# Summing four gate-weight tiles on GpSimd earlier in the start-up of a hybrid attention layer, and bunching the other four

## The chip, the cores and the metric

The kernel runs on one core of a Trainium2 chip. The metric is device time in microseconds (us) from the first to the last instruction of a launch with what the runtime adds around it; lower is better. Of the kernel before there are three timed runs and one profiled execution.

The engines are named as the profile names them: PE is TensorE (matrix products; PEld is its weight load), DVE is VectorE, ACT is ScalarE, POOL is GpSimd, and SP is the engine that issues most DMAs. Each works through its own instructions in a fixed order and waits on semaphores.

## The reference

One post-norm residual sub-layer over `x` of 1024 rows by 1024 columns, all in float32. A conditioning vector `c` gives shift, scale and a residual gate; the normalised rows go through one wide projection, then through eight heads of forgetting attention and eight of stick-breaking attention, and back through an output projection. What matters here is the gate:

```
mod = silu(c) @ w_ada + b_ada
shift, scale, gate = mod[:, :D], mod[:, D:2*D], mod[:, 2*D:]
u = layer_norm(x) * (1 + scale) + shift
h = u @ w_in                      # q, k, v, g of both head groups
...                               # two kinds of attention, gated by silu(g)
resid = ALPHA * x + gate * (y @ w_out)
out = layer_norm(resid, ln_g, ln_b)
```

The gate is a vector of 1024 numbers: the product of `silu(c)` (1024 long) and a 1024 by 1024 block of `w_ada`. It is first needed when the output weights are scaled by it, far into the kernel.

## The kernel before

**Products.** Every product is made of three float32r products: the operands are split into a high part and a rest (hi and lo), and hi times hi, hi times lo and lo times hi are summed in PSUM. PE is the engine with the most work.

**Start-up.** The input projection of the first head pair and the q and k of the second is written out by hand. The five outputs in `START` (named q0, k0, g0, q1, k1 in the tiles) are computed in two passes: a first pass over rows 0 to 511, and a second pass over rows 512 to 1023. In the second pass `late_round(kb)` (L717) transposes a block of normalised rows on PE, ACT writes its high part `uh` (L219) and the modulated block itself (L220), and DVE the rest `ul` (L223). `start_steps` (L558) then runs three products per weight tile (L567, L568, L571). The first two accumulators, both halves of `late_acc` and named `st_late` in the profile (q and k of pair 0), are filled together (L740). The third (`st_g0b`), fourth (`st_q1b`) and fifth (`st_k1b`) are filled one after the other by the loop at L749. Each accumulator is read out by `evac_m` in two halves of heads: ACT rounds a q or k half (L232, L241), DVE takes the rest (L233, L244), and for k an SP DMA copies the half to the other partitions (L243). Within one accumulator these steps alternate: an ACT half waits for the DVE half before it.

**The gate.** `load_gate(kt)` (L689) fetches one of eight weight tiles of 128 rows by 1024 columns (`wg`, 512 KB) into the pool `att`, which has six buffers and holds the input rows `x` before and the attention tiles `kp` and `be` after. `gate_term(kt, h)` (L693) adds `silu(c)` times one half (512 columns) of a tile to the tile `gate`. Half 0 goes over ACT (scale, L698) and POOL (add, L699); half 1 is one DVE instruction (L701); for tile 0 ACT writes both halves (L696). The loads of tiles 0 to 3 are issued during the second pass (L742), and those of tiles 4 to 7 in the loop at L749, one every three steps. The eight terms themselves also stand in that loop, at every third of its 24 steps, under `after(*rounded)`, which lets them be placed only behind the last rounding of the second pass. At L713 one product then sums `gate` over the partitions.

**What sets the order.** PE and SP follow the order in which the code is written up to L767, and PE to the end. The orders of ACT, DVE and POOL, and of SP after L767, are chosen ahead of time by a scheduler, so a changed line can move instructions elsewhere.

**What follows.** The first attention units run beside the projection of v for rows 512 on: scores `S` (L411, L412), of which there is one buffer; ACT makes `kp` and `be` from it (L430, L431); DVE scans `kp` (L436); POOL clears one column of `be` and multiplies (L443, L442); PE transposes `be` (L459). Beside it POOL splits fetched weights into `whi` (L125) and `wlo` (L126): `v_2b` and `v_3b` for the v projection, then `2_0` and `2_1` (the g weights of pair 1).

Of the kernel before, what the change touches and what calls it, by code (L numbers as in the profile page):

```python
# [10 lines left out]
AF = mybir.ActivationFunctionType  # L11
ALU = mybir.AluOpType
# [4 lines left out]
NB = 8  # L17
# [10 lines left out]
def tile_hybrid_layer(  # L28
# [17 lines left out]
    nc = tc.nc  # L46
# [9 lines left out]
    def att_tile(name, dt=F32):  # L56
        return big("att", 6, name, dt)
# [15 lines left out]

    RING = 5
    WARM = (4, 1, 1, 1, 1)
    GEARLY = 8
    NORM_ON = {6: nc.vector, 7: nc.vector}
    FROW = 12
    SPACE = 5
# [2 lines left out]
    def after(*instructions):  # L82
        stack = ExitStack()
        for i in instructions:
            stack.enter_context(tc.issue_after(i.ins))
        return stack
# [17 lines left out]
    gate = cp.tile([P, D], F32, tag="gate", name="gate")  # L104
# [53 lines left out]
    sc = cp.tile([P, NB], F32, tag="sc", name="sc")  # L158
# [113 lines left out]
    def evac_m(p, m, ch, acc, heads=(0, 1)):  # L272
        if m == 0:
            evac_q(p, ch, acc, qst[p], heads)
        elif m == 1:
            return evac_k(p, ch, acc, kst[p], klo[p], heads)
        else:
            evac_g(p, ch, acc, sgt[p])
# [279 lines left out]
    def start_steps(ns, accs, kb, a=0, b=512, parts=(0, 1)):  # L558
        s = slice(a, b)
        w = {}  # L560
        for n in ns:
            hi, lo = split[("k", kb) if n < NW else ("h", kb // 4)]
            at = n if n < NW else kb % 4
            w[n] = hi[:, at * P:at * P + P], lo[:, at * P:at * P + P]
        if 0 in parts:
            for n in ns:
                nc.tensor.matmul(accs[n], w[n][0], u_hi[kb][:, s], start=(kb == 0), stop=False)  # L567
                nc.tensor.matmul(accs[n], w[n][1], u_hi[kb][:, s], start=False, stop=False)  # L568
        if 1 in parts:
            for n in ns:  # L570
                nc.tensor.matmul(accs[n], w[n][0], u_lo[kb][:, s], start=False, stop=(kb == NB - 1))  # L571
# [115 lines left out]
    wg = {}  # L687

    def load_gate(kt):  # L689
        wg[kt] = att_tile(f"wg_{kt}")  # L690
        nc.sync.dma_start(wg[kt], w_gate[kt])

    def gate_term(kt, h):  # L693
        s = slice(h * 512, h * 512 + 512)
        if kt == 0:
            nc.scalar.activation(gate[:, s], wg[kt][:, s], AF.Copy, scale=sc[:, 0:1])  # L696
        elif h == 0:
            nc.scalar.activation(wg[kt][:, s], wg[kt][:, s], AF.Copy, scale=sc[:, kt:kt + 1])  # L698
            nc.gpsimd.tensor_tensor(gate[:, s], gate[:, s], wg[kt][:, s], op=ALU.add)  # L699
        else:  # L700
            nc.vector.scalar_tensor_tensor(gate[:, s], wg[kt][:, s], sc[:, kt:kt + 1], gate[:, s],  # L701
                                           op0=ALU.mult, op1=ALU.add)
# [14 lines left out]
    def late_round(kb):  # L717
        u_turn(kb, 512, 1024)
        return u_round(kb, 512, 1024), u_rest(kb, 512, 1024)
# [17 lines left out]
    for kb in range(NB):  # L737
        if kb + 2 < NB:
            rounded = late_round(kb + 2)
        start_steps(range(2), acc1, kb, 512, 1024)  # L740
        if kb < 4:
            load_gate(kb)  # L742
        if kb < len(evacs):
            n, h = evacs[kb]
            with after(*rounded):
                evac_m(*START[n], 0, acc0[n], (h,))
    acc1 += [pv_tile("st_g0b", True), pv_tile("st_q1b"), acc_tile("st_k1b")]
    v0_w.update((n, fetch_w(f"v0_{n}b", w_v[0, n], 512)) for n in (2, 3))
    for n in range(5):  # L749
        if n >= 2:  # L750
            for kb in range(NB):
                start_steps((n,), acc1, kb, 512, 1024)
                step = (n - 2) * NB + kb
                if step % 3 == 1 and step // 3 < GEARLY:
                    with after(*rounded):
                        gate_term(step // 3, 0)
                        gate_term(step // 3, 1)
                    if step // 3 < 4:
                        load_gate(step // 3 + 4)
        last_evac = evac_m(*START[n], 1, acc1[n])  # L760
        if n == 2:
            floor.append(ps.tile([P, 512], F32, tag="fl", bufs=1, name="floor"))
            nc.vector.memset(floor[0][:, :512 - P], 0.0)
            nc.scalar.copy(floor[0][:, 512 - P:], ident)
# [282 lines left out]
```

## Time and profile before

| | us |
|---|---|
| timed runs, lowest / median / highest of 3 | 698.71 / 699.13 / 699.32 |
| profiled execution, its own time | 699.99 |
| its span, first to last instruction | 698.2 |
| PE busy in the span | 676.0 (97%) |
| POOL busy | 410.6 (59%) |
| DVE busy | 483.7 (69%) |
| ACT busy | 385.0 (55%) |

A line of the timeline gives the start, the duration (of a run of equal instructions: from the first start to the last end), the engine, the line of the kernel, the operation, the tiles written and read, the shapes and the count, and in brackets how long the engine had been idle and what released it. A line of the chain of waits gives a start, a duration and what the chain went through. The rows that carry the argument are in the prediction.

### The profile page before, as it was taken

How to read it: one execution, taken by the hardware profiler on the slowest of the kernel's cores; microseconds unless marked ns; L12 is line 12 of the kernel's file. 1: busy time of each engine (PE TensorE's matmuls, PEld its weight loads, DVE VectorE, ACT ScalarE, POOL GpSimd, SP SyncE). 2: the span in 40 equal slices, each digit the busy share in tenths (PEclk: the TensorE clock that was granted, in tenths of full speed). 3: DMA queues.
4: the chain of work that ended last, by engine and by line, in shares of the span. 5: the costliest groups of instructions: out<-in, count | busy, mean ns of one | idle time of the engine just before them, and what ended most of it. 6: DMA issues, size and time to landing. Idle time of an engine off the chain costs nothing.

```text
span 698.2 us, 11781 instructions
## 1 busy us (share of the span) xinstructions
PE 676.0 (97%) x4033; PEld 589.0 (84%) x4033; DVE 483.7 (69%) x931; ACT 385.0 (55%) x866; POOL 410.6 (59%) x530
## 2 busy tenths in 40 slices
PE   7999989999999999999999999999999999999995
PEld 4789887888997888889988877889988889888884
DVE  5985678767657676767686684758576767784644
ACT  5667567856658576666664554645564666531000
POOL 4560487656437566556388897868483464665412
PEclk9999999999999999999999999999999999999998
DMA  8953451112102122112144554345241299143301
GB/s 313 415 215 128 113 176 53 28 39 49 42 9 69 40 53 55 38 46 61 29 134 145 174 164 155 112 116 164 95 143 51 58 283 364 56 162 113 119 31 60
DMA packets 44027, 81.59 MB, mean 117 GB/s; under 512 B 5120, under 2 KB 18880, under 8 KB 43072
## 3 DMA queue, kind: packets, MB, share of 16 engines
q1 hardware_dynamic: 42816, 76.65, 33.5%
q10 hardware_dynamic: 1152, 4.19, 2.0%
q8 instruction: 32, 0.52, 0.3%
q14 instruction: 27, 0.22, 0.1%
HBM read 60.34 MB, written 16.29 MB: 110 GB/s over the span
## 4 chain that ended last, share of the span: by engine, by line
PE 76%; DVE 7%; DMA 5%; POOL 4%; ACT 4%; issue 3%; SPq 0%; POOLq 0%; DVEq 0%; ACTq 0%
PE pv L474 9%; PE m L256 8%; PE m L257 8%; PE m L258 8%; PE T L459 8%; PE o L835 4%; PE o L833 4%; PE o L834 4%; PE S L412 4%; PE S L411 4%; PE v L311 3%; PE v L313 3%; PE v L312 3%; DMA wss<-in_w_ss_dram 1%; DMA raw<-in_w_qkg_dram 1%
## 5 line engine op out<-in xcount | busy, mean ns | idle before, releaser
L256 PE MATMUL m<-uh,whi 128*128 128x512 f32 x304 | 126.3, 415 | 0.5 <-DVE kl L244 0.5
L257 PE MATMUL m<-ul,whi 128*128 128x512 f32 x304 | 119.8, 394 | 0.0
L258 PE MATMUL m<-uh,wlo 128*128 128x512 f32 x304 | 119.6, 394 | 0.0
L462 DVE TENSOR_TENSOR pt<-T,pt 128x512 fp32r<-128x512 f32 (+2 forms) x192 | 100.6, 550 | 16.1 <-ACT pt L461 14.9
L442 POOL TENSOR_TENSOR be<-be,kp 128x127 f32<-128x127 f32 (+3 forms) x64 | 77.1, 1205 | 34.9 <-DVE kp L440 25.9
L461 ACT CAST pt<-T 128x512 fp32r<-128x512 f32 (+2 forms) x192 | 85.7, 480 | 17.2 <-PE T L459 13.6
L436 DVE TENSOR_TENSOR_SCAN kp<-kp,floor 128x512 f32<-128x512 f32 (+2 forms) x64 | 65.2, 1018 | 32.4 <-ACT kp L430 31.4
L474 PE MATMUL pv<-pt,v 128*128 128x256 f32 (+3 forms) x640 | 81.7, 272 | 3.8 <-DVE pt L462 3.8
L474 PEld LDWEIGHTS pv<-pt,v 128*128 128x128 f32 (+1 forms) x640 | 77.4, 163 | 9.0 <-DVE pt L462 4.7
L425 POOL TENSOR_SCALAR a<-a,l 128x1024 f32<-128x1024 f32 (+3 forms) x64 | 48.3, 755 | 43.8 <-DVE l L424 31.2
L423 ACT ACTIVATE a<-a,nm 128x1024 f32<-128x1024 f32 (+3 forms) x64 | 49.8, 778 | 40.5 <-DVE nm L418 40.1
L258 PEld LDWEIGHTS m<-uh,wlo 128*128 128x128 f32 x304 | 57.1, 188 | 13.5
L411 PE MATMUL S<-k,q 128*128 128x512 f32 (+5 forms) x192 | 66.6, 348 | 1.5 <-ACT be L431 0.8
L412 PE MATMUL S<-kl,qz 128*128 128x512 f32 (+5 forms) x192 | 65.5, 342 | 0.0
L256 PEld LDWEIGHTS m<-uh,whi 128*128 128x128 f32 x304 | 57.3, 188 | 9.2 <-DVE kl L244 0.9
L257 PEld LDWEIGHTS m<-ul,whi 128*128 128x128 f32 x304 | 57.4, 189 | 8.0
L495 POOL TENSOR_TENSOR ty<-ty,sg 64x256 f32<-64x256 f32 x64 | 47.7, 745 | 26.5 <-DVE ty L494 12.5
L418 DVE CUSTOM_DVE_ANT_0 a<-S,fb 128x1024 f32<-128x1024 f32 (+3 forms) x64 | 48.2, 754 | 15.9 <-PE S L412 7.8
L430 ACT ACTIVATE kp<-S 128x128 f32<-128x128 f32 (+3 forms) x64 | 41.7, 651 | 31.9 <-PE S L412 28.6
L311 PE MATMUL v<-whi_v,uh 128*128 128x256 f32 (+1 forms) x192 | 56.0, 292 | 0.7 <-DVE kl L244 0.7
L389 ACT CAST qz<-q 64x128 fp32r<-64x128 f32 x128 | 37.4, 295 | 31.3 <-PE S L412 30.0
L313 PE MATMUL v<-wlo_v,uh 128*128 128x256 f32 (+1 forms) x192 | 54.2, 282 | 0.0
(284 smaller groups left out, 1628.6 us busy)
## 6 DMA issues: line engine op xcount, KB each, us to landing
raw<-in_w_qkg_dram SPq DMA_DIRECT2D x38, 256.0 KB, 3.0
wss<-in_w_ss_dram SPq DMA_DIRECT2D x7, 1024.0 KB, 9.0
x<-in_x_dram SPq DMA_DIRECT2D x8, 512.0 KB, 7.1
k<-k SPq DMA_DIRECT2D x32, 128.0 KB, 2.3
wg<-in_w_gate_dram SPq DMA_DIRECT2D x8, 512.0 KB, 5.0
raw_o<-in_w_out_dram SPq DMA_DIRECT2D x16, 256.0 KB, 2.7
fb<-f_dr ACTq DMA_DIRECT2D x8, 512.0 KB, 4.3
wo_dr<-whi_o SPq DMA_DIRECT2D x16, 256.0 KB, 2.4
```

The source lines that it names most:

```text
L256: nc.tensor.matmul(acc, hi[:, c], u_hi[kt][:, s], start=(kt == 0), stop=False)
L257: nc.tensor.matmul(acc, hi[:, c], u_lo[kt][:, s], start=False, stop=False)
L258: nc.tensor.matmul(acc, lo[:, c], u_hi[kt][:, s], start=False, stop=(kt == NB - 1))
L311: nc.tensor.matmul(acc[:, :n], u_hi[kt][:, ts_], hi[:, s], start=(kt == 0), stop=False)
L313: nc.tensor.matmul(acc[:, :n], u_hi[kt][:, ts_], lo[:, s], start=False, stop=(kt == NB - 1))
L411: nc.tensor.matmul(S[:, s, :w], qst[p][h][:, qs], kst[p][h][:, ks], start=True, stop=False)
L412: nc.tensor.matmul(S[:, s, :w], z, klo[p][:, ks], start=False, stop=True)
L436: nc.vector.tensor_tensor_scan(rv, rv, floor[0][:, 512 - n:][:, ::-1], initial=0.0, op0=ALU.mult, op1=ALU.max)
L442: nc.gpsimd.tensor_tensor(be[:, :ke - 1], be[:, :ke - 1], kp[:, 1:ke], op=ALU.mult)
L461: nc.scalar.copy(hi[:, :n, qo:qo + P], t3)
L462: nc.vector.tensor_tensor(lo[:, :n, qo:qo + P], t3, hi.bitcast(F32)[:, :n, qo:qo + P], op=ALU.subtract)
L474: nc.tensor.matmul(acc[:m, q0:256], vt[p][:, kb, h * P:h * P + m], pt[:, kb % 4, q0:], start=start, stop=stop)
```

## The change

The terms of tiles 0 to 3 move from ACT, DVE and POOL to POOL alone, and stand right behind their loads in the second pass. Tile 0 is scaled into `gate`; tiles 1 to 3 are scaled in place and then added, half by half. The terms of tiles 4 to 7 stay on ACT, POOL and DVE as before, and now stand in the steps of the third accumulator alone (every second of its eight steps), each right behind the load of its tile. The constant `GEARLY` goes.

```
-    GEARLY = 8
...
     def gate_term(kt, h):
         s = slice(h * 512, h * 512 + 512)
         if kt == 0:
-            nc.scalar.activation(gate[:, s], wg[kt][:, s], AF.Copy, scale=sc[:, 0:1])
+            nc.gpsimd.tensor_scalar(gate[:, s], wg[kt][:, s], sc[:, 0:1], 1.0, op0=ALU.mult, op1=ALU.mult)
+        elif kt < 4:
+            nc.gpsimd.tensor_scalar(wg[kt][:, s], wg[kt][:, s], sc[:, kt:kt + 1], 1.0, op0=ALU.mult, op1=ALU.mult)
+            nc.gpsimd.tensor_tensor(gate[:, s], gate[:, s], wg[kt][:, s], op=ALU.add)
         elif h == 0:
             nc.scalar.activation(wg[kt][:, s], wg[kt][:, s], AF.Copy, scale=sc[:, kt:kt + 1])
             nc.gpsimd.tensor_tensor(gate[:, s], gate[:, s], wg[kt][:, s], op=ALU.add)
...
         if kb < 4:
             load_gate(kb)
+            gate_term(kb, 0)
+            gate_term(kb, 1)
...
                 start_steps((n,), acc1, kb, 512, 1024)
-                step = (n - 2) * NB + kb
-                if step % 3 == 1 and step // 3 < GEARLY:
+                if n == 2 and kb % 2 == 0:
+                    load_gate(kb // 2 + 4)
                     with after(*rounded):
-                        gate_term(step // 3, 0)
-                        gate_term(step // 3, 1)
-                    if step // 3 < 4:
-                        load_gate(step // 3 + 4)
+                        gate_term(kb // 2 + 4, 0)
+                        gate_term(kb // 2 + 4, 1)
```

The order on PE stays the same from end to end. In the changed kernel the line numbers up to the gate are lower by one and those behind it higher by two (by up to four within the start-up loops). The numbers at the ends of the tile names are buffers and differ from program to program.

DVE before, from the last round of the second pass to the read-out of the fifth accumulator's first half (`wg_714` to `wg_750` are tiles 1 to 3, `wg_831` and `wg_845` tiles 4 and 5):

```order
L223 TENSOR_TENSOR ul_127<-xT_512_772,uh_119 128x512
L701 SCALAR_TENSOR_TENSOR gate<-wg_714,sc,gate 128x512
L701 SCALAR_TENSOR_TENSOR gate<-wg_732,sc,gate 128x512
L701 SCALAR_TENSOR_TENSOR gate<-wg_750,sc,gate 128x512
L233 SCALAR_TENSOR_TENSOR q_0_246<-st_late,q_0_246 64x512
L233 SCALAR_TENSOR_TENSOR q_1_247<-st_late,q_1_247 64x512
L244 TENSOR_TENSOR kl_250<-st_late,k_0_248 64x512
L250 SCALAR_TENSOR_TENSOR sg_550<-sg_550,st_g0b 128x512
L244 TENSOR_TENSOR kl_250<-st_late,k_1_249 64x512
L763 MEMSET floor 128x384
L701 SCALAR_TENSOR_TENSOR gate<-wg_831,sc,gate 128x512
L701 SCALAR_TENSOR_TENSOR gate<-wg_845,sc,gate 128x512
```

DVE now, the same place (`wg_840` and `wg_851` are tiles 4 and 5):

```order
L222 TENSOR_TENSOR ul_127<-xT_512_786,uh_119 128x512
L232 SCALAR_TENSOR_TENSOR q_0_246<-st_late,q_0_246 64x512
L232 SCALAR_TENSOR_TENSOR q_1_247<-st_late,q_1_247 64x512
L243 TENSOR_TENSOR kl_250<-st_late,k_0_248 64x512
L243 TENSOR_TENSOR kl_250<-st_late,k_1_249 64x512
L249 SCALAR_TENSOR_TENSOR sg_550<-sg_550,st_g0b 128x512
L765 MEMSET floor 128x384
L703 SCALAR_TENSOR_TENSOR gate<-wg_840,sc,gate 128x512
L703 SCALAR_TENSOR_TENSOR gate<-wg_851,sc,gate 128x512
```

The three terms between the last `ul` and the first read-out of `st_late` are gone, and the second half of k now stands ahead of `sg`. ACT changes at the same places: its five gate instructions ahead of that read-out are gone, the second half of k stands ahead of `sg`, and `wg_851` stands ahead of the read-out of `st_q1b` where tile 5 stood behind its first half.

POOL before, from the last row statistics to the splits of the v weights:

```order
L173 TENSOR_TENSOR rs_a_519<-rs_a_519,mhalf 128x1
L699 TENSOR_TENSOR gate<-gate,wg_714 128x512
L699 TENSOR_TENSOR gate<-gate,wg_732 128x512
L699 TENSOR_TENSOR gate<-gate,wg_750 128x512
L125 TENSOR_SCALAR whi_v_2b<-raw_v_2b 128x512
L125 TENSOR_SCALAR whi_v_3b<-raw_v_3b 128x512
```

POOL now:

```order
L172 TENSOR_TENSOR rs_a_519<-rs_a_519,mhalf 128x1
L695 TENSOR_SCALAR gate<-wg_696,sc 128x512 x2
L697 TENSOR_SCALAR wg_716<-wg_716,sc 128x512 x2
L698 TENSOR_TENSOR gate<-gate,wg_716 128x512 x2
L697 TENSOR_SCALAR wg_738<-wg_738,sc 128x512 x2
L697 TENSOR_SCALAR wg_760<-wg_760,sc 128x512 x2
L698 TENSOR_TENSOR gate<-gate,wg_738 128x512 x2
L698 TENSOR_TENSOR gate<-gate,wg_760 128x512 x2
L124 TENSOR_SCALAR whi_v_2b<-raw_v_2b 128x512
```

Three instructions between the statistics and `whi_v_2b` have become fourteen, none of which waits for ACT any more. From `whi_v_2b` to the first unit's `be` the row is the same as before, with tiles 4 to 7 in the same places. SP keeps its order up to the fifth accumulator; behind that, one fetch of a weight tile (`raw_0_0`) moves ahead of a k copy.

## Prediction

> **What bounds the kernel now.** I read the page first, then PE's waits, then PE's timeline where it waited, and from there backwards along the chain.
>
> ```profile
> PE 676.0 (97%) x4033; PEld 589.0 (84%) x4033; DVE 483.7 (69%) x931; ACT 385.0 (55%) x866; POOL 410.6 (59%) x530
> ...
> PE T L459 <- DVE pt L462: 1.3, 3, 0.9
> PE T L459 <- POOL be L443: 1.1, 1, 1.1
> PE S L411 <- ACT be L431: 0.8, 1, 0.8
> ```
>
> PE is busy 676.0 of 698.2 us, and the change takes nothing from PE. So it can gain only where PE stands still, and lose only where PE comes to stand still. Two of PE's waits come once each, and both lie right behind the gate terms. PE's timeline there:
>
> ```profile
> 74.51 0.63 PE L571 MATMUL st_late<-ul,hw 128*128 128x512 f32 x2
> 86.17 0.40 PE L567 MATMUL st_k1b<-uh,whi_st 128*128 128x512 f32 x1
> 91.52 0.39 PE L571 MATMUL st_k1b<-ul,hw 128*128 128x512 f32 x1
> 94.59 0.28 PE L312 MATMUL v<-whi_v_3b,ul 128*128 128x256 f32 x1
> ...
> 94.71 0.28 PE L313 MATMUL v<-wlo_v_3b,uh 128*128 128x256 f32 x1
> 95.78 0.38 PE L411 MATMUL S<-k,q 128*128 128x256 f32 x1 [0.78 <-ACT be L431]
> 97.57 0.34 PE L411 MATMUL S<-k,q 128*128 128x384 f32 x1
> 97.75 0.34 PE L412 MATMUL S<-kl,qz 128*128 128x384 f32 x1
> 99.19 0.33 PE L459 MATMUL T<-ident,be 128*128 128x128 f32 x1 [1.11 <-POOL be L443]
> ```
>
> Matmuls overlap, so what a wait costs is read between starts. The products of v start 0.12 us apart (94.59, 94.71). The score would have started at 94.83 and started at 95.78: 0.95 us. The second score product starts 0.18 behind the first (97.57, 97.75); by the same step the transpose would have started at 97.93 and started at 99.19: 1.26 us. Together 2.21 us. From the last start of `st_late` at 74.51 up to 94.71 PE waits for nothing; its other waits behind this come from DVE and move along with it.
>
> Why are these two late? The chain of waits, from the loads of tiles 4 to 7 on:
>
> ```profile
> 83.65 4.79 DMA wg<-in_w_gate_dram
> 88.54 1.30 DVE gate L701
> 89.87 0.69 DVE q L233
> ...
> 91.84 0.72 ACT wg L698
> 94.37 1.27 POOL gate L699
> 97.45 1.29 POOL wlo L126
> 98.78 0.36 POOL be L442
> ```
>
> Tile 5 lands at 88.44, its DVE term holds up the q half on DVE, that the other q half on ACT, that ACT's scaling of tiles 6 and 7, that POOL's last gate sum, and that the splits ahead of `be`. The score hangs on the same chain: ACT and DVE reach the fifth accumulator late.
>
> ```profile
> 92.57 0.58 ACT L241 CAST k<-st_k1b 64x512 fp32r<-64x512 f32 x1
> 92.31 1.61 DVE L701 SCALAR_TENSOR_TENSOR gate<-wg,sc,gate 128x512 f32<-128x512 f32 x1
> 93.95 0.68 DVE L244 TENSOR_TENSOR kl<-st_k1b,k 64x512 fp32r<-64x512 f32 x1
> ```
>
> PE is done with `st_k1b` at 91.91 (91.52 + 0.39), but ACT takes k only at 92.57 and DVE, in tile 7's term until 93.92, at 93.95. The first unit's `kp` and `be` on ACT follow, and behind them PE's score, which needs their buffer.
>
> **The change, part by part.**
>
> *Tiles 0 to 3 on POOL.* When can they run, what do they cost, and who waits behind them?
>
> ```profile
> 52.23 2.16 SPq L691 DMA_DIRECT2D wg<-in_w_gate_dram  x4
> DMA to landing us min/median/max: 4.1/5.0/6.8
> L425 POOL TENSOR_SCALAR a<-a,l 128x512 f32<-128x512 f32 x8 | 5.5, 692 | 5.5 <-DVE l L424 5.5
> 74.85 4.73 POOL L699 TENSOR_TENSOR gate<-gate,wg 128x512 f32<-128x512 f32 x3 [23.30 <-ACT wg L698]
> 81.53 0.62 POOL L125 TENSOR_SCALAR whi_v_2b<-raw_v_2b 128x512 fp32r<-128x512 f32 x1 [1.94 <-PE st_q1b L571]
> ```
>
> Eight scalings with a pointer at 0.69 us (the same operation and size at L425) are 5.5 us. Six sums are 7.6 us at the 1.27 us of one that ran alone (94.37), 9.5 us at the 1.58 us of the three that ran beside DVE's gate terms. In all 13.1 to 15.0 us. From the first landing (52.23 + 5.0 = 57.2) they end at 70 to 72; the load issued last, at about 54, lands by 61 at the slowest, long before its turn. Before the change POOL stands idle for 23.30 us up to 74.85, so this costs nothing. Behind it in POOL's queue stands `whi_v_2b`, which waits for PE until 81.53 anyway: 9 us of cover are left. If that cover went, the splits for v would be late, of which PE reads `v_3b` around 94.6.
>
> *ACT and DVE freed behind the second pass.*
>
> ```profile
> 75.90 0.58 ACT L232 ACTIVATE q<-st_late 64x512 fp32r<-64x512 f32 x1
> 74.20 4.22 DVE L701 SCALAR_TENSOR_TENSOR gate<-wg,sc,gate 128x512 f32<-128x512 f32 x3 [0.56 <-ACT gate L696]
> 78.45 0.68 DVE L233 SCALAR_TENSOR_TENSOR q<-st_late,q 64x512 fp32r<-64x512 f32 x1
> 81.85 0.58 ACT L241 CAST k<-st_late 64x512 fp32r<-64x512 f32 x1 [0.26 <-DVE kl L244]
> 83.01 1.98 SPq L691 DMA_DIRECT2D wg<-in_w_gate_dram  x4
> ```
>
> DVE's three terms (4.22 us) held the first q rest until 78.45. Without them it follows PE's end of `st_late` (74.51 + 0.63 = 75.14) and one ACT half of about 0.6: 75.75, which is 2.7 us sooner. The alternation behind it is unchanged, so the last k half starts 2.7 sooner too, and with it the k copy on SP and the loads of tiles 4 to 7, which SP issues right behind it: 80.3 instead of 83.01. Their buffers are free by then (POOL ends at 72 at the latest). Tile 5 lands at 85.7.
>
> *Tiles 4 to 7.* Their instructions are the same. DVE's chain, 2.7 us sooner, ends at 93.92 - 2.7 = 91.2; its q half, at 89.87 before, could start at 87.2, and the accumulator that it reads is done by then, since PE begins the next one, `st_k1b`, at 86.17. So `st_k1b` finds ACT and DVE free at 91.91. ACT takes k then, and DVE its rest one ACT half later, 0.6 us, at 92.55. From the start of that k rest to the score it took 1.83 us (93.95 to 95.78): the buffer is free at 94.4, and PE comes at 94.83. The 0.95 us are gone, with 0.4 to spare.
>
> POOL's last gate sum comes to 91.7, its splits end (98.74 - 2.7) at 96.0, and the first `be` at 96.5 at the latest; PE comes to its transpose at 97.93 - 0.95 = 96.98. The 1.26 us are gone as well, with 0.5 to spare. What is late next is nothing on PE until DVE's waits, which come behind unchanged orders and move along with PE.
>
> [...]
>
> ```profile
> 29.97 6.49 POOL L556 TENSOR_TENSOR hw<-raws,hw 128x512 fp32r<-128x512 f32 x5 [5.03 <-ACT hw L555]
> 33.50 0.68 DVE L223 TENSOR_TENSOR ul<-xT_early,uh 128x512 fp32r<-128x512 f32 x1
> 34.10 1.13 DVE L206 TENSOR_TENSOR modc<-modc,bss_sb 128x2 f32<-128x2 f32 x1
> 38.55 0.15 DVE L206 TENSOR_TENSOR modc<-modc,bss_sb 128x2 f32<-128x2 f32 x1
> 72.94 0.69 DVE L223 TENSOR_TENSOR ul<-xT,uh 128x512 fp32r<-128x512 f32 x1 [0.64 <-ACT xT L220]
> ```
>
> A sum of two SBUF columns takes 1.13 us beside POOL and 0.15 without it: DVE is held. But `ul`, which reads PSUM and SBUF, takes 0.68 in the midst of POOL's 6.49 us and 0.69 where POOL is idle. In the second pass every DVE instruction reads PSUM, so I take 0 for the holding. [...]
>
> *The sum.* -0.95 - 1.26 = -2.21 us. The profiled execution took 699.99, so one like it would take 697.8. It stands 0.86 above the median of 699.13; by that median, 696.9.
>
> **The rivals.**
>
> *The loads gain nothing.* Tiles 4 to 7 land when they did, because the transfers or the buffers and not SP's place set them. Then ACT, which now has tile 5 ahead of the q half, and DVE run the old chain and both waits stay: 699.1. Or they land half as early, and the score's 0.4 and the transpose's 0.5 of room are used up: something between, such as 698.2 with only the transposes' wait or 697.9 with only the score's gone. Also here: what PE gains is waited away behind 100 us. For: rows of DMA and engine waits mix in that chain. Against: SP issued the four loads right behind the k copies, at 83.01, and the chain begins with them. 0.22.
>
> *DVE is held in the second pass.* This is the case slower than before: POOL's sums hold DVE's PSUM reads as they hold L206.
>
> ```profile
> 57.00:61.00 4.00, 4.00 (x36) 4.00 (x36) 1.18 (x3) 3.20 (x6) 0.00 (x0) 1.00 0.62 252
> 61.00:73.00 12.00, 12.00 (x67) 10.03 (x66) 7.91 (x14) 11.36 (x20) 0.00 (x0) 1.00 0.08 18
> ```
>
> From 57 to 73 DVE is busy 1.18 + 7.91 = 9.1 us, so it has 6.9 idle. If DVE and POOL only took turns, 13.1 to 15.0 us of POOL would make DVE's last `ul` 6.2 to 8.1 us late; it ends at 73.63 and PE reads it at 74.51, so 0.88 is cover, and PE is 5.3 to 7.2 late. Less 2.21 that is 3.1 to 5.0 slower, 702.2 to 704.1. It is slower than before only once DVE is held more than 6.9 + 0.88 + 2.21 = 10 us. Against it stands the 0.68 at 33.50. 0.07.
>
> *More is gained.* PE's three waits for DVE at transposes, 1.3 us in all, come later; with POOL and ACT ahead of their old times DVE could be ahead too and spare PE these: 699.13 - 2.21 - 1.3 = 695.6. Against: DVE's queue there is as before, and it waits for PE in its turn. 0.06.
>
> That the change doesn't do what it says is the first rival's lower end.
>
> **How the numbers follow.** The forecast has 0.65: 696.9. About 0.2%, 1.4 us, is what a measurement of this kernel can tell from no change. Faster by more than that are the forecast and the last rival, 0.71; within it lies the first rival, 0.22; slower is the held DVE, 0.07. The range takes in the last rival below and the first one above to its end: 695.6 to 699.1. What is left out is the slower case and what I have not thought of.
>
> **What would show it.** Right: POOL's fourteen terms lie between 57 and 72 with nothing waiting for them; DVE's `ul` stay at 0.69; the first q rest of `st_late` starts near 75.8 and SP's loads of tiles 4 to 7 near 80.3; ACT takes k of `st_k1b` near 92.0; PE's two waits are off its list, and its later ones are as before. Wrong: `ul` longer than 0.7 while POOL sums; tile 5 landing later than 87; a score or transpose of the first units that still waits; or a new wait on PE behind 100 that takes the 2.2 us back.

## The result, and the profile after

The changed kernel takes 697.59 us in the median of nine runs (695.96 to 698.42); the kernel before, beside it, took 699.13 (697.66 to 700.05, nine runs). The ratio is 0.9976 with a 95% interval of 0.9965 to 0.9987: 1.5 us less, between 0.9 and 2.4 us. The profiled execution of the changed kernel took 697.78 us, with a span of 695.8.

PE's waits, of the changed kernel (what waited for what, total us, times, longest):

```profile
PE pv L473 <- DVE pt L461: 3.6, 4, 1.6
...
PE T L458 <- DVE pt L461: 1.4, 3, 0.9
...
PE S L410 <- DVE nm L417: 0.5, 1, 0.5
```

The score's wait for ACT's `be` and the transpose's wait for POOL's `be` are not on the list any more. PE's timeline at the place (line numbers are now one lower than those of the prediction):

```profile
92.24 0.39 PE L570 MATMUL st_k1b<-ul,hw 128*128 128x512 f32 x1
...
95.43 0.29 PE L312 MATMUL v<-wlo_v_3b,uh 128*128 128x256 f32 x1
95.55 0.28 PE L410 MATMUL S<-k,q 128*128 128x256 f32 x1
...
97.39 0.34 PE L411 MATMUL S<-kl,qz 128*128 128x384 f32 x1
97.57 0.27 PE L458 MATMUL T<-ident,be 128*128 128x128 f32 x1
...
103.22 1.02 PE L715 MATMUL gate<-gate,half 128*128 128x512 f32 x2
```

The score now starts 0.12 us behind the product ahead of it, and the transpose 0.18 behind the second score product: PE runs through. From the last product of `st_k1b` to the transpose it is 5.33 us (97.57 - 92.24), where it was 7.67 (99.19 - 91.52): 2.34 us less.

POOL's timeline of the changed kernel, with the terms of tiles 0 to 3 first:

```profile
56.62 1.37 POOL L695 TENSOR_SCALAR gate<-wg,sc 128x512 f32<-128x512 f32 x2 [4.35 <-DMA wg<-in_w_gate_dram]
58.60 1.37 POOL L697 TENSOR_SCALAR wg<-wg,sc 128x512 f32<-128x512 f32 x2 [0.62 <-DMA wg<-in_w_gate_dram]
59.93 2.57 POOL L698 TENSOR_TENSOR gate<-gate,wg 128x512 f32<-128x512 f32 x2
62.47 2.70 POOL L697 TENSOR_SCALAR wg<-wg,sc 128x512 f32<-128x512 f32 x4
65.12 5.07 POOL L698 TENSOR_TENSOR gate<-gate,wg 128x512 f32<-128x512 f32 x4
82.25 0.62 POOL L124 TENSOR_SCALAR whi_v_2b<-raw_v_2b 128x512 fp32r<-128x512 f32 x1 [12.05 <-PE st_q1b L570]
...
96.65 0.40 POOL L441 TENSOR_TENSOR be<-be,kp 128x127 f32<-128x127 f32 x1
```

The terms end at 70.19 (65.12 + 5.07) and POOL then idles 12.05 us until PE lets it go on: they are wholly covered. DVE beside them (grouped over 56.5 to 70.2 us), and then DVE, SP and ACT on the way to the score:

```profile
L222 DVE TENSOR_TENSOR ul<-xT,uh 128x512 fp32r<-128x512 f32 x6 | 4.1, 691 | 4.8 <-ACT xT L219 4.8
```

```profile
76.51 0.68 DVE L232 SCALAR_TENSOR_TENSOR q<-st_late,q 64x512 fp32r<-64x512 f32 x1 [2.16 <-ACT q L231]
...
93.28 0.68 DVE L243 TENSOR_TENSOR kl<-st_k1b,k 64x512 fp32r<-64x512 f32 x1 [1.49 <-ACT k L240]
```

```profile
81.07 1.98 SPq L690 DMA_DIRECT2D wg<-in_w_gate_dram  x4
```

```profile
86.41 0.73 ACT L700 ACTIVATE wg<-wg,sc 128x512 f32<-128x512 f32 x1 [0.81 <-DMA wg<-in_w_gate_dram]
...
92.67 0.58 ACT L240 CAST k<-st_k1b 64x512 fp32r<-64x512 f32 x1 [2.21 <-PE st_k1b L570]
```

`ul` stays at 691 ns. The k half and its rest now wait for PE and for each other, not for gate terms. All these times stand about 0.7 us later than the prediction's. The shift is there from this execution's first product of `st_q` on, which lies ahead of anything that the change touches.

### The profile page after: what moved, and what is told of

Its sections match the earlier page's. It is cut to its first block, busy times and chain, and to the rows that moved or that the text cites. A ratio compares the mean times of both kernels' runs of the same rounds, so it can differ in the third digit from the quotient of the medians.

```text
span 695.8 us, 11785 instructions
## 1 busy us (share of the span) xinstructions
PE 674.9 (97%) x4033; PEld 589.1 (85%) x4033; DVE 477.3 (69%) x928; ACT 382.3 (55%) x861; POOL 420.0 (60%) x541
## 4 chain that ended last, share of the span: by engine, by line
PE 82%; DMA 5%; DVE 5%; POOL 3%; issue 2%; ACT 2%; SPq 0%; POOLq 0%; DVEq 0%; ACTq 0%
PE pv L473 9%; PE m L255 8%; PE m L256 8%; PE m L257 8%; PE T L458 8%; PE o L837 4%; PE o L835 4%; PE o L836 4%; PE S L411 4%; PE S L410 4%; PE v L310 4%; PE v L311 4%; PE v L312 4%; DMA wss<-in_w_ss_dram 3%; DMA raw<-in_w_qkg_dram 1%
## 5 line engine op out<-in xcount | busy, mean ns | idle before, releaser
L460 ACT CAST pt<-T 128x512 fp32r<-128x512 f32 (+2 forms) x192 | 85.7, 480 | 17.2 <-PE T L458 13.7
```

Of the source, the lines that this page charges most:

```text
L460: nc.scalar.copy(hi[:, :n, qo:qo + P], t3)
```

## The experiments

The theory was this: the gain is PE's two waits and nothing else, it comes from the first half of the change (DVE and ACT freed behind the second pass, loads earlier) and it holds because POOL's terms have cover. The rivals: the bunching of tiles 4 to 7 matters too; the freed DVE alone or the earlier loads alone would do; POOL's sums would be as good anywhere; the terms still cost something that isn't a wait at these places. Besides, it was open why less was timed than the place shows. The kernel before, run again beside each group, took 699.38 us (e1 to e4, 29 runs) and 699.65 (e5 to e8, 17 runs).

| kernel | median us | ratio to before, 95% |
|---|---|---|
| the change | 697.59 | 0.9976 (0.9965 to 0.9987) |
| e1, first half alone | 697.42 | 0.9977 (0.9967 to 0.9987) |
| e2, second half alone | 701.52 | 1.0038 (1.0024 to 1.0053) |
| e3, three half terms back on DVE | 700.94 | 1.0023 (1.0013 to 1.0034) |
| e4, loads 4 to 7 later | 699.23 | 0.9999 (0.9988 to 1.0009) |
| e5, seven eighths of the gate left out | 697.07 | 0.9968 (0.9955 to 0.9981) |
| e6, all tiles on POOL | 702.97 | 1.0053 (1.0041 to 1.0065) |
| e7, change and causal mask on POOL | 695.13 | 0.9942 (0.9930 to 0.9955) |
| e8, before once more | 699.23 | 0.9993 (0.9983 to 1.0003) |

**e1, the first half alone.** Tiles 0 to 3 early on POOL, tiles 4 to 7 at their old steps:

```
-                if n == 2 and kb % 2 == 0:
-                    load_gate(kb // 2 + 4)
+                step = (n - 2) * NB + kb
+                if step % 3 == 1 and step // 3 < 4:
+                    load_gate(step // 3 + 4)
+                if step % 3 == 1 and step // 3 >= 4:
...
```

> Tiles 0 to 3 summed on POOL in the second pass as in the changed kernel; the loads and terms of tiles 4 to 7 at their old steps. My theory (both PE waits go because ACT, DVE and POOL come free earlier behind the second pass; where tiles 4 to 7 stand in the code adds nothing, since SP issues their loads behind the k copies either way): PE's two waits at the first score and the first transpose stay away (0 and 0), the loads of tiles 4 to 7 are issued near 81, time as the changed kernel, 697.6 within 1. Rival (bunching the other four is what gains): the loads stay where they were relative to the fifth accumulator, both waits are back, 0.8 and 1.1 us, time 699.1.

697.42 us, neither of the two waits, and the same 5.33 us from the last `st_k1b` product to the transpose (97.39 - 92.06). On every engine this kernel has the instructions of the change in the same order, so it is a second set of runs of the same program. Beside the first half the bunching does nothing: the order comes out the same with and without it.

**e2, the second half alone.** Tiles 0 to 3 stay on three engines behind the second pass, and tiles 4 to 7 are bunched:

```
-                step = (n - 2) * NB + kb
-                if step % 3 == 1 and step // 3 < GEARLY:
+                if n == 2 and kb % 2 == 0:
                     with after(*rounded):
...
+                        gate_term(kb // 2, 0)
+                        gate_term(kb // 2, 1)
+                    load_gate(kb // 2 + 4)
+                    with after(*rounded):
+                        gate_term(kb // 2 + 4, 0)
+                        gate_term(kb // 2 + 4, 1)
```

> Tiles 0 to 3 stay on ACT, POOL and DVE behind the second pass; tiles 4 to 7 are loaded and summed within the steps of the third accumulator. My theory: seven DVE terms and, on POOL, five sums now stand between the floor and the first units; DVE's run of terms from 85 (seven at 0.75 to 1.7, two q rests) ends at 92 to 98, so the first score waits 0.5 to 4 us and the transpose 0 to 2; time 699 to 702, not faster than before. Rival (bunching is what gains): no waits, 697.6.

701.52, slower than the kernel before. PE's timeline, then DVE's, of e2:

```profile
98.03 0.58 PE L411 MATMUL S<-k,q 128*128 128x256 f32 x1 [3.00 <-ACT be L431]
```

```profile
91.51 4.67 DVE L701 SCALAR_TENSOR_TENSOR gate<-wg,sc,gate 128x512 f32<-128x512 f32 x4
96.21 0.68 DVE L244 TENSOR_TENSOR kl<-st_k1b,k 64x512 fp32r<-64x512 f32 x1
```

Four of DVE's terms stand right ahead of the k rest that the score hangs on, and the wait of 0.78 becomes 3.00. So the bunching is not what gains. The sign of the whole change rests on its first half.

**e3, half 1 of tiles 1 to 3 back on DVE.** The loads stay where the change has them, and so does POOL's half 0:

```
-        elif kt < 4:
+        elif kt < 4 and h == 0:
...
-            gate_term(kb, 1)
+            if kb == 0:
+                gate_term(kb, 1)
...
+                if n == 2 and kb in (0, 2, 4):
+                    with after(*rounded):
+                        gate_term(kb // 2 + 1, 1)
```

> The changed kernel with half 1 of tiles 1 to 3 back on DVE behind the second pass; POOL keeps tile 0 and half 0 of tiles 1 to 3 early, ACT stays free, the loads of tiles 4 to 7 stay early. One DVE term then stands ahead of the first q rest, where DVE idles 2 us, and five ahead of the last q rests. My theory (the queue of DVE terms in front of the fifth accumulator decides): DVE comes to the k rest 1 to 2 us late, the first score waits about 1.2 us (0.5 to 2), the transpose 0 to 0.5; time about 698.8. Rival (it is the earlier landing of tiles 4 to 7 that counts, and that is unchanged here): no waits, 697.6.

700.94 where 698.8 was expected, with a wait at the score of 1.98 us where 1.2 was expected. PE's timeline, then DVE's, of e3:

```profile
92.25 0.39 PE L570 MATMUL st_k1b<-ul,hw 128*128 128x512 f32 x1
...
97.71 0.39 PE L410 MATMUL S<-k,q 128*128 128x256 f32 x1 [1.98 <-ACT be L430]
...
107.04 1.02 PE L715 MATMUL gate<-gate,half 128*128 128x512 f32 x2
```

```profile
94.04 1.81 DVE L703 SCALAR_TENSOR_TENSOR gate<-wg,sc,gate 128x512 f32<-128x512 f32 x1
95.89 0.68 DVE L243 TENSOR_TENSOR kl<-st_k1b,k 64x512 fp32r<-64x512 f32 x1
```

DVE takes the k rest at 95.89 in place of 93.28, behind a gate term that lasts 1.81 us beside POOL. So early loads alone are not enough: DVE has to be free as well. The place costs 3.81 us against the change (107.04 - 92.25 = 14.79 from the last `st_k1b` to the gate product, against 103.22 - 92.24 = 10.98), nearly twice the wait. Of this, 2.15 us are lost by the start of the score (97.71 - 92.25 = 5.46, against 95.55 - 92.24 = 3.31). The other 1.66 fit PE's clock, in e3's table by stage (the last four columns: POOL, granted clock, DMA share, GB/s):

```profile
98.00:99.00 1.00, 1.00 (x10) 1.00 (x10) 0.81 (x3) 0.69 (x3) 1.00 (x3) 1.00 0.56 176
99.00:100.00 1.00, 1.00 (x7) 1.00 (x6) 0.63 (x2) 0.31 (x2) 0.76 (x3) 0.59 0.89 277
100.00:101.00 1.00, 1.00 (x5) 0.90 (x5) 0.00 (x0) 0.33 (x1) 0.14 (x1) 0.50 0.31 58
...
103.00:104.00 1.00, 1.00 (x9) 0.87 (x8) 0.29 (x1) 0.64 (x2) 1.00 (x3) 1.00 0.00 0
```

In finer slices the clock stands at 0.50 from about 99.2 to 102.6; 3.4 us at half speed lose 1.7 us, by estimate.

**e4, loads 4 to 7 later.** The change with two unread loads of 512 KB ahead of them on SP:

```
+                if n == 2 and kb == 0:
+                    for i in range(2):
+                        nc.sync.dma_start(att_tile(f"extra_{i}"), w_gate[i])
```

> The changed kernel with two more loads of 512 KB, which nothing reads, issued ahead of those of tiles 4 to 7: these land some 3 us later, about as late as before the change, while ACT, DVE and POOL stay free behind the second pass. My theory (tile landings start the chain of terms): DVE ends tile 7's term near 94.4, the first score waits 0.7 us (0.3 to 1.5), the transpose 0 to 0.5; time about 698.3. Rival (the freed engines alone count, the landing does not): no waits, 697.6. Old chain in full: both waits, 699.1.

699.23 where about 698.3 was expected, and part of the score's wait is back. PE's timeline, then ACT's and DVE's, of e4:

```profile
91.98 0.39 PE L570 MATMUL st_k1b<-ul,hw 128*128 128x512 f32 x1
...
95.90 0.39 PE L410 MATMUL S<-k,q 128*128 128x256 f32 x1 [0.45 <-ACT be L430]
...
103.80 1.02 PE L715 MATMUL gate<-gate,half 128*128 128x512 f32 x2
```

```profile
91.22 0.72 ACT L700 ACTIVATE wg<-wg,sc 128x512 f32<-128x512 f32 x1 [0.53 <-DMA wg<-in_w_gate_dram]
```

```profile
89.67 4.37 DVE L703 SCALAR_TENSOR_TENSOR gate<-wg,sc,gate 128x512 f32<-128x512 f32 x3
94.08 0.68 DVE L243 TENSOR_TENSOR kl<-st_k1b,k 64x512 fp32r<-64x512 f32 x1
```

ACT waits for the last tile to land, and the k rest starts 2.10 us behind the last `st_k1b` product (94.08 - 91.98), where it was 1.04 (93.28 - 92.24). So the loads' time does set the chain: freeing DVE alone is not enough either. The place shows 0.84 us against the change (103.80 - 91.98 = 11.82, against 10.98), but the median stands 1.6 above it. What the other 0.8 is stays open: the two loads also take buffers and transfer time (4.4 us from issue to landing in the median; the loads of tiles 4 to 7 take 6.7 here and 5.2 in the change), and 0.16 of it lies outside the span (time less span is 2.18 us in the median of e4's runs, 2.02 in the change's).

**e5, the bound.** Loads and terms of tiles 1 to 7 left out:

```
-        if kb < 4:
+        if kb < 1:
...
-                if n == 2 and kb % 2 == 0:
-                    load_gate(kb // 2 + 4)
...
```

> The changed kernel without the loads and terms of weight tiles 1 to 7: seven eighths of the gate are left out, tile 0 stays. It is a bound on what any placement of these terms can gain. Theory (the gate terms cost PE nothing any more once the two waits are gone): the same as the change, 697.5 (696.7 to 698.2), no wait at the first score and transpose, and the first transpose 5.3 us behind the last start of st_k1b, as in the change. Rival (the terms or their 4 MB of loads still cost something that is not a wait at these two places, by contention behind 100 us): under 696.5.

697.07, its interval overlapping the change's. PE's timeline of e5:

```profile
91.52 0.39 PE L570 MATMUL st_k1b<-ul,hw 128*128 128x512 f32 x1
...
96.85 0.27 PE L458 MATMUL T<-ident,be 128*128 128x128 f32 x1
```

Again 5.33 us: with seven tiles gone PE is no sooner at its transpose than with them on POOL. The runs show nothing that another placement of these terms could still gain (by the median span, e5 is 0.25 us below the change, 695.35 against 695.6).

**e6, all tiles on POOL.** ACT and DVE do no gate work at all:

```
-        elif kt < 4:
+        elif kt < 8:
```

> The changed kernel with tiles 4 to 7 on POOL too, so that ACT and DVE do no gate work at all. Theory (only POOL's cover made its sums free; here it has none): from 86.1, where its splits for v end, POOL has eight scalings (5.5 us), four sums (5.1), two splits' high parts (1.2) and one low part (1.3) ahead of the first be, which ends at about 99.6 in place of 97.0; PE comes to its transpose at 97.6 and waits 2.0 us there (1 to 4), and perhaps again for the second be behind three more of POOL's long instructions; no wait at the score. With the slower clock behind such a wait 700.6 (698.6 to 703.5). Rival (ACT's and DVE's share was what cost, POOL has time enough): no wait, 697.5 or less.

702.97, the slowest of all, and inside the expected range, but the main wait came at another place. PE's timeline, then POOL's and ACT's, of e6:

```profile
91.98 0.39 PE L570 MATMUL st_k1b<-ul,hw 128*128 128x512 f32 x1
...
99.53 0.44 PE L410 MATMUL S<-k,q 128*128 128x384 f32 x1 [2.42 <-ACT be L430]
...
99.99 0.29 PE L458 MATMUL T<-ident,be 128*128 128x128 f32 x1
...
107.69 1.02 PE L715 MATMUL gate<-gate,half 128*128 128x512 f32 x2
```

```profile
97.40 1.29 POOL L125 TENSOR_TENSOR wlo<-raw,whi 128x512 fp32r<-128x512 f32 x1
98.62 0.44 POOL L441 TENSOR_TENSOR be<-be,kp 128x127 f32<-128x127 f32 x1
```

```profile
99.09 0.38 ACT L430 ACTIVATE be<-S 128x256 f32<-128x256 f32 x1 [1.24 <-POOL be L441]
```

POOL's first `be` starts at 98.62 in place of 96.65. ACT's next `be`, of the second unit, waits for it and holds the one buffer of scores, and PE waits for that buffer at the third unit's score (128x384), one step ahead of the transpose that I had named; at the fourth unit's score it waits 0.51 us more. The place costs 4.73 us against the change (107.69 - 91.98 = 15.71, against 10.98). POOL is a good place only where it has cover.

**e7, the causal mask on POOL.** The records had shown something else, behind 400 us. DVE, then POOL, of the changed kernel:

```profile
403.08 3.22 DVE L395 TENSOR_TENSOR fb<-fb,causal 128x128 f32<-128x128 f32 x1
...
408.80 0.29 DVE L395 TENSOR_TENSOR fb<-fb,causal 128x128 f32<-128x128 f32 x1
```

```profile
402.61 1.29 POOL L122 TENSOR_TENSOR raw_o<-raw_o,gate 128x512 f32<-128x512 f32 x1
403.89 1.01 POOL L424 TENSOR_SCALAR a<-a,l 128x896 f32<-128x896 f32 x1
404.87 1.29 POOL L125 TENSOR_TENSOR wlo_o<-raw_o,whi_o 128x512 fp32r<-128x512 f32 x1
```

The same sum of two SBUF tiles takes 0.29 us at 408.80 (the median of the 64 is 0.33) and 3.22 at 403.08, while POOL runs back to back, and DVE's whole queue stands behind it. So, in the changed kernel:

```
-            nc.vector.tensor_tensor(f[:, dg], f[:, dg], causal, op=ALU.add)
+            nc.gpsimd.tensor_tensor(f[:, dg], f[:, dg], causal, op=ALU.add)
```

> The changed kernel with the sum of the forget bias and the causal mask (two SBUF inputs, 128x128) on POOL in place of DVE. On DVE it took 0.28 us in the median but 3.22 at 403 us, beside POOL's back-to-back work, and PE waited behind it. Theory (DVE is held there and PE's time behind 400 us varies with it): about 1 us less than the change, 696.6 (695.6 to 697.2), and no such sum on DVE. Rival (POOL's queue makes the mask late, so DVE waits for POOL): 698 to 701.

695.13 us (694.61 to 695.86): about 2.4 below the change (0.9942 and 0.9976 of the kernel before), and below the expected range; it beats both kernels. By the median span it is 2.2 below (693.4 against 695.6). The sums on POOL (instructions; ns min, median, max; first and last start), then PE's waits, of e7:

```profile
L395 POOL TENSOR_TENSOR fb<-fb,causal x64: 448/462/472, 350.1 to 614.2; 128x128 f32<-128x128 f32 x64
```

```profile
PE pv L473 <- DVE pt L461: 2.1, 2, 1.7
```

Each takes 0.46 us, and PE's wait for `pt` falls from 3.6 to 2.1 us. DVE now waits for POOL's mask 4.1 us in all, but that reaches PE little. Against the changed kernel's execution PE runs level within 0.2 us up to 411, is 2.0 ahead at 431 and 2.4 at the end. Two things stay open. e1's execution, with the sums on DVE, gains 1.2 us between 408 and 431 as well, so the medians and not this pair give the size. And the edit takes all 64 sums (36 us in the changed kernel) off DVE, so the held sum and the shorter queue are not told apart.

**e8, the kernel before once more.**

> The kernel before once more, compared with itself: ratio 1.000 within 0.0015. The profile shows what varies from one execution to another: theory, both waits are there again (0.6 to 1.0 at the score, 0.9 to 1.3 at the transpose), the first transpose 7.7 us behind the last start of st_k1b within 0.2; the start up to the first product of st_q (15.04 and 15.74 so far) and the stretch behind 400 us differ by up to 1 us without any edit. Rival (the start moves with the edit): 15.0 again, within 0.1.

Ratio 0.9993 (0.9983 to 1.0003): the comparison adds no difference of its own. PE's timeline of e8:

```profile
16.18 0.51 PE L567 MATMUL st_q<-uh,whi_st 128*128 128x512 f32 x1
...
92.20 0.39 PE L571 MATMUL st_k1b<-ul,hw 128*128 128x512 f32 x1
...
96.23 0.39 PE L411 MATMUL S<-k,q 128*128 128x256 f32 x1 [0.55 <-ACT be L431]
...
99.66 0.33 PE L459 MATMUL T<-ident,be 128*128 128x128 f32 x1 [1.12 <-POOL be L443]
```

Both waits are there again; the score's, 0.55, is just under the 0.6 to 1.0 that was expected. The transpose starts 7.46 us behind the last `st_k1b` product (99.66 - 92.20), where it was 7.67 and 7.5 to 7.9 was expected. So the place gains 2.1 to 2.3 us, by which execution of the kernel before one takes. The first `st_q` product, at 15.04 in the first execution of this kernel, starts at 16.18 in this one: the start moves by a microsecond without any edit, and the changed kernel's 15.74 lies in between.

## Why the prediction was right

**PE's two waits, 2.21 us.** Right, and the size too: 2.34 us on the trace. Against the shift of 0.72 us with which this execution came to the place, the score gained 0.95 (predicted 0.95) and the transpose 1.39 (predicted 1.26). Most of the difference is that the first matmul behind the score's wait took 0.38 us where the same one now takes 0.28. e5 shows that this is all that the place has.

**Tiles 0 to 3 on POOL.** Right: 56.6 to 70.2 us, 13.1 us of work (the low end of 13.1 to 15.0), with 12.05 us of cover behind them where 9 were counted as the least. Holding of DVE: none, `ul` at 0.69. The rival in which DVE is held fell; e6 shows the loss that comes when POOL's cover is gone.

**ACT, DVE and the loads sooner.** Right. Less the 0.72 us of the later start, the q rest comes at 75.8 (predicted 75.75), SP's loads at 80.35 (80.3), tile 5 is taken at 85.7 (85.7), and the k rest at 92.56 (92.55). e3 and e4 each take away one of the two, the free DVE or the early loads, and each brings the score's wait back. So the first rival, in which the loads gain nothing, fell as well.

**Tiles 4 to 7 bunched.** The prediction gave this nothing of its own; e1 confirms it.

**What follows behind 100 us.** Here the prediction was too sure that PE's later waits "move along", and its sum left out what the runtime adds around the span. The medians moved by 1.54 us, not 2.2; e1's, of the same program, by about 1.6 (0.9977 of 699.38). The interval still holds 2.2.

About 0.3 us of the difference lies outside the span. The time less the span is 1.96 to 2.08 us in every run of the change and of e1, but 1.67 to 1.80 in every run of the kernel before whose span is recorded, and in e2, e3 and e5 to e8. No run shows why. By the median span alone e1 gains 2.2 us (695.4 against 697.6), as much as the two waits were worth.

The rest is blurred by what differs without any edit: the start, by up to 1.1 us between executions of the kernel before, and the stretch from 408 to 431 us, by as much. In e5 PE comes 0.7 us sooner than in the changed kernel up to 408 and 0.2 later at 431; e1, with the order of the change, gains 1.2 there against it. That all of the gain is waited away behind 100 us, as the first rival also had it, fell: the interval ends at 0.9. Whether some of the 2.34 is systematically given back there is open: the intervals don't tell. That the profiled execution took 697.78 us where the sum had 697.8 is luck: it started 0.7 late and made that up behind 404 us. The prediction lays all of PE's later waits to DVE; one of them, 0.2 us at a transpose, came from POOL.

**More is gained.** PE's waits for `pt` at the transposes stayed (1.3 before, 1.4 after), so that rival fell.

## What to carry to other kernels

Moving work to an idle engine pays by what it takes off the queue that a bound engine waits for, and only while the move has cover: the same sums on POOL gained 1.5 us with 12 us of idle time behind them and lost 3.7 (1.0053 of 699.65) when all eight tiles' terms were there and the last four stood among the splits and `be`. When an edit's waits are gone, leaving the work out altogether tells at once whether any further placement is worth trying. An instruction whose longest time is ten times its median (3.22 us against 0.33) is worth following up: here the move that came of it gained more than the change (2.4 us against 1.5).

## What the runs showed of the hardware that was not expected

**A place with a PE wait of 1.98 us cost 3.81.** That is e3. The granted clock falls to 0.50 about 1.5 us after PE has resumed (97.71), and is back at 1.00 by 103; the products of v meanwhile start 0.21 us apart in place of 0.12. In e6 it falls to 0.50 about 0.6 us behind the end of a wait of 2.42 and stays there as long (100.1 to 103.5). In e2 it falls at 97.0, while PE still waits its 3.00 us, and stays halved about twice as long, to 103.8. Behind the waits of 0.78 and 1.11 in the kernel before, and 0.45 in e4, it stays at 1.00. No run shows what sets when it falls and when it is back.

**A sum on DVE took far longer than any one POOL instruction beside it.** A sum of two SBUF tiles that takes 0.33 us in the median took 3.22 in the changed kernel, and one of 0.35 took 4.15 in the kernel before, both across several POOL instructions that ran without a gap and took 1.29 us at the longest; `ul`, which reads PSUM, took 0.68 to 0.69 every time in both. That POOL's work held the sum is an inference from these rows; no run shows by what means.
